# The passage from the first attention to its FFN in a written order on three engines: the context's part first, four modulation rows moved into the FFN

## The chip, the cores and the metric

The kernel runs on one core of a Trainium2 chip. The metric is the device time of one execution in microseconds (us); less is better. A run of the kernel on the chip gives one time; the time of a kernel is the median of its runs. A profiled execution is a further one, with its own time.

The engines of the core that matter here: PE (TensorE, matmuls into the PSUM memory; PEld is its weight load), DVE (VectorE), ACT (ScalarE), POOL (GpSimd) and SP (SyncE, which issues most transfers). Each works through its own queue in order, and engines wait for one another by semaphores.

## What is computed

A trunk of two layers over 512 latent tokens (x) and 256 context tokens (ctx) of width 1024. Cut to what matters:

```
for layer in range(2):
    mod_x = six vectors of 1024 from silu(c) @ ada_w[layer] + ada_b[layer]
    mod_c = six vectors of 1024 from silu(c_ctx) @ ada_w[layer] + ada_b[layer]
    h = rmsnorm(x) * (1 + mod[1]) + mod[0]          # for x and for ctx
    o = attention(h)                                # concatenated heads @ w_out
    x = x + mod_x[2] * o_x ;  ctx = ctx + mod_c[2] * o_c
    h = rmsnorm(x) * (1 + mod[4]) + mod[3]          # for x and for ctx
    x = x + mod_x[5] * ((silu(h_x @ w1) * (h_x @ w3)) @ w2)
    ctx = the same with h_c and mod_c[5]            # in layer 0 only
return rmsnorm(x) * final_g
```

The change touches layer 0 between `o = attention(h)` and the first products with w1 and w3.

## The kernel before

Activations lie transposed: a tile has 128 of the 1024 features on the partitions and the tokens along the free axis, so x is eight tiles of 128x512 (`xr`) and the context eight of 128x256 (`cr`). Every factor of a large product is split into a high and a low part, `hi` and `lo = src - hi`, and the product is three matmuls per 128 features (`mm3`, L209 to L211): high by high, high by low, low by high. The normalised inputs are `hx[k]` and `hc[k]`, each with its two parts (`xh`, `xl`, `ch`, `cl`); together they are `hb`. A weight tile of 128x1024 is loaded by SP (`raw`), copied to its high part by ACT (L160) and subtracted for the low part by DVE (L161); there are three buffers each of raw, high and low tiles. The class `Stream` (`S`) keeps the weights in one list and loads and splits them in that order, some ahead of their use.

Most of the program is put in order on the engines by the framework's scheduler: it takes the instructions in the order in which the program names them as a priority, and lets a later one go first on an engine that would otherwise stand still. `tc.issue_after` puts one instruction behind another on its engine. In a region of `manual_schedule` the named engines keep the written order of the region's instructions; the kernel before has one such region, at its start (lines 76 to 961).

**The end of the attention.** The attention's results of the eight units pass through `prep(m)`, which splits them into `hx[m]` and `hc[m]` (L1291, L1292, and `split`, L198 and L199, for the context). The output projection with `wo_ab` is done in two halves of four features tiles each. The first half (`first_part`, `wo_chunk(.., 0)`) lies among the attention's steps. The second half, `wo_chunk(m, w, "x" or "c", 4)` for m from 0 to 7, is twelve matmuls into one of two PSUM buffers (`lin`) and then one DVE instruction that adds the result times mod[2] to the residual (L1313). In the kernel before the x chunks come first, with the context's chunks of m = 0 and 1 among them, and the other six chunks of the context (`held`) after the x norm.

**The norms.** `sq_sum` squares the eight tiles on ACT (L331, L334) and adds them up in two accumulators, on DVE (L340) for even and on POOL (L338) for three odd ones. `rstd_of` sums over the features by a matmul with ones (L308), and makes 1/sqrt by Ln, Exp and a Newton step on ACT and DVE (L315 to L320). `h_make` makes one tile of the input of the FFN: a DVE product (L352), ACT's high part with the shift (L353), DVE's low part (L354).

**The modulation rows.** `ada_rows` makes one 128-feature piece of a modulation vector from a row tile of 128x1024 (512 KB, loaded by SP): two DVE instructions with a running sum (L271, L272), one for x and one for the context. In layer 0 the vectors 2 to 4 and the first half of vector 5 are made in the attention, four of these rows (vector 5, k = 0 to 3, `late_rows`) in this passage; the second half of vector 5 and all of layer 1 follow in the FFN through `rows(n, after)`, with two row buffers that SP fills again as they come free (`ada_request`, L623). Vector 5 is first used by the residual sums of the FFN (`to_residual`, L1553).

**The start of the FFN.** `plain_tile(0)` runs 16 small matmuls without use for the result (`keep_busy`, L219), and then w1 and w3 of the first 128 hidden features: x with w1, x with w3, then the context with both, each 8 x 3 matmuls. The table of ACT's functions is changed to Silu behind the context's last tile (`silu_tables`, L291). The FFN works on 22 hidden tiles: four plain ones (p = 0 and 1, two each), and nine pairs by a scheme of seven products in place of eight (`seven`, L1518 to L1520), with sums of tokens and weights that DVE makes (`token_sums`, `first_sum`), and the products with w2 (`down`, L1559 to L1561).

## Time and profile before

| | us |
|---|---|
| median of 3 runs (1594.85 to 1597.19) | 1596.67 |
| the profiled execution's own time | 1602.4 |
| its span, first to last instruction | 1600.6 |
| PE busy / DVE busy / ACT busy / POOL busy in the span | 1546.4 / 1245.5 / 738.3 / 261.2 |
| the passage and the first FFN tile in the span | about 420 to 487 |

How to read the lines that follow. A row of the timeline gives the start (us from the span's start), the time that it took, engine, line of the kernel, operation, `out<-in` by tile names, the shapes and the count, and in brackets how long the engine stood idle before it and for whom it waited. A row of a group gives line, engine, operation, names, shapes, count, then busy us and mean ns of one. A row of the windows gives from:to, the length, busy us (and count) of PE, PEld, DVE, ACT and POOL, the granted clock of PE (1.00 is full speed), the share of the 16 DMA engines and GB/s. Matmuls are pipelined: a matmul of 512 columns is shown with 0.39 us, while the next starts 0.23 us after it.

### The profile page before, as it was taken

The numbers are of one execution on the slowest core, as the hardware profiler recorded it, in microseconds if no ns is written. First come the engines' busy times: TensorE is split into PE (matmuls) and PEld (weight loads), VectorE is DVE, ScalarE is ACT, GpSimd is POOL, SyncE is SP. The second block draws the span as 40 slices with busy tenths as digits, with TensorE's granted clock in tenths as the row PEclk, the third lists the DMA queues.
The fourth block names the chain that finished last, engine by engine and source line by source line (L and its number), as shares of the span: only waits on it lengthen the run. The fifth ranks groups of instructions, "written<-read, shape, count | busy, mean of one in ns | idle before, by whom it ended". The sixth has DMA issues, their size and how long they took to land.

```text
span 1600.6 us, 25584 instructions
## 1 busy us (share of the span) xinstructions
PE 1546.4 (97%) x9904; PEld 1381.6 (86%) x9904; DVE 1245.5 (78%) x2135; ACT 738.3 (46%) x1280; POOL 261.2 (16%) x303
## 2 busy tenths in 40 slices
PE   8899998999999999999999999998998999999997
PEld 5798887877878999989999998886777899989896
DVE  4768797966698799879788867677766987869686
ACT  4546554445344423423424254456664543525354
POOL 1032223463010000000100001253431000000001
PEclk9999999999999999999999999999999999999998
DMA  9322253542245465575866752320002342423321
GB/s 357 105 60 81 77 166 125 182 139 87 63 132 158 119 182 158 135 208 160 213 180 165 200 148 71 106 67 27 28 27 65 120 145 72 130 73 96 119 80 53
DMA packets 68449, 195.28 MB, mean 122 GB/s; under 512 B 6772, under 2 KB 19220, under 8 KB 68328
## 3 DMA queue, kind: packets, MB, share of 16 engines
q1 hardware_dynamic: 58136, 159.95, 30.8%
q0 software_dynamic: 9184, 32.39, 9.6%
q8 instruction: 78, 1.28, 0.3%
q10 hardware_dynamic: 1008, 1.31, 0.2%
q14 instruction: 43, 0.35, 0.1%
HBM read 160.45 MB, written 4.86 MB: 103 GB/s over the span
## 4 chain that ended last, share of the span: by engine, by line
PE 58%; DVE 6%; DMA 3%; issue 2%; ACT 1%; POOL 0%; DVEq 0%; ACTq 0%; POOLq 0%; SPq 0%
PE f L1520 4%; PE f L1519 4%; PE f L1518 4%; PE f L1950 4%; PE f L1949 4%; PE f L1948 4%; PE f L1561 3%; PE f L1560 3%; PE f L1559 3%; PE f L210 3%; PE f L211 3%; PE f L209 3%; PE f L2001 2%; PE f L2002 2%; PE f L2003 2%
## 5 line engine op out<-in xcount | busy, mean ns | idle before, releaser
L198 ACT ACTIVATE wh<-raw 128x1024 fp32r<-128x1024 f32 (+1 forms) x96 | 92.3, 978 | 232.1 <-DVE raw L539 99.4
L209 PE MATMUL lin<-hb,wh 128*128 128x512 f32 (+1 forms) x440 | 157.2, 358 | 6.0 <-ACT hb L1291 3.1
L210 PE MATMUL lin<-hb,wh 128*128 128x512 f32 (+1 forms) x440 | 154.8, 352 | 0.5 <-DVE hb L1292 0.5
L211 PE MATMUL lin<-hb,wl 128*128 128x512 f32 (+1 forms) x440 | 154.4, 351 | 0.0
L199 DVE TENSOR_TENSOR wl<-raw,wh 128x1024 fp32r<-128x1024 f32 (+1 forms) x96 | 107.2, 1123 | 36.3 <-ACT wh L198 34.2
L271 DVE SCALAR_TENSOR_TENSOR junk<-raw,tables 128x1024 bf16<-128x1024 f32 x80 | 100.0, 1250 | 18.4 <-DMA raw<-in_ada_wT_dram 18.1
L204 POOL DMA_DIRECT2D wl<-raw x39 | 34.1, 874 | 445.3 <-ACT wl L203 388.4
L1559 PE MATMUL f<-g,wh 128*128 128x512 f32 (+1 forms) x304 | 102.8, 339 | 0.0
L1560 PE MATMUL f<-g,wh 128*128 128x512 f32 (+1 forms) x304 | 102.8, 339 | 0.0
L1949 PE MATMUL f<-hb,wh 128*128 128x256 f32 x360 | 101.7, 283 | 0.0
L1948 PE MATMUL f<-hb,wh 128*128 128x256 f32 x360 | 101.4, 283 | 0.0
L1950 PE MATMUL f<-hb,wl 128*128 128x256 f32 x360 | 101.2, 283 | 0.0
L1561 PE MATMUL f<-g,wl 128*128 128x256 f32 (+1 forms) x304 | 100.8, 336 | 0.2 <-DMA wl<-raw 0.2
L209 PEld LDWEIGHTS lin<-hb,wh 128*128 128x128 f32 x440 | 83.2, 189 | 20.4 <-ACT hb L1291 3.5
L1520 PE MATMUL f<-hb,wl 128*128 128x384 f32 x288 | 96.3, 334 | 0.2 <-DMA wl<-raw 0.2
L1518 PE MATMUL f<-hb,wh 128*128 128x384 f32 x288 | 96.3, 334 | 0.0
L1519 PE MATMUL f<-hb,wh 128*128 128x384 f32 x288 | 96.2, 334 | 0.0
L210 PEld LDWEIGHTS lin<-hb,wh 128*128 128x128 f32 x440 | 83.3, 189 | 11.1 <-DVE hb L1292 0.6
L211 PEld LDWEIGHTS lin<-hb,wl 128*128 128x128 f32 x440 | 83.3, 189 | 10.4
L161 DVE TENSOR_TENSOR wl<-raw,wh 128x1024 fp32r<-128x1024 f32 x57 | 74.0, 1300 | 16.0 <-ACT wh L160 14.0
L160 ACT CAST wh<-raw 128x1024 fp32r<-128x1024 f32 x57 | 59.7, 1050 | 57.0 <-PE t L210 15.0
L338 POOL TENSOR_TENSOR ns_a<-ns_a,ns_s 128x256 f32<-128x256 f32 (+1 forms) x12 | 12.2, 1018 | 420.8 <-ACT ns_s L334 414.2
(442 smaller groups left out, 4870.9 us busy)
## 6 DMA issues: line engine op xcount, KB each, us to landing
raw<-in_w_dram SPq DMA_DIRECT2D x132, 512.0 KB, 3.6
raw<-in_ada_wT_dram SPq DMA_DIRECT2D x80, 512.0 KB, 3.9
wl<-raw POOLq DMA_DIRECT2D x39, 512.0 KB, 6.3
raw<-in_w_ab_dram SPq DMA_DIRECT2D x24, 512.0 KB, 4.2
raw<-in_ada_w_dram SPq DMA_DIRECT2D x12, 512.0 KB, 9.3
raw<-in_w_c_dram SPq DMA_DIRECT2D x12, 512.0 KB, 3.7
nb<-in_na_bias_dram POOLq DMA_DIRECT2D x16, 256.0 KB, 3.3
raw<-in_wo_ab_dram SPq DMA_DIRECT2D x8, 512.0 KB, 3.5
```

Of the source, the lines that this page charges most:

```text
L209: nc.tensor.matmul(ps, wh(k), xh(k), start=k == 0, stop=False)
L210: nc.tensor.matmul(ps, wh(k), xl(k), start=False, stop=False)
L211: end = nc.tensor.matmul(ps, wl(k), xh(k), start=False, stop=k == n - 1)
L1518: nc.tensor.matmul(ps, wh(k), b[:, 0, :], start=k == 0, stop=False)
L1519: nc.tensor.matmul(ps, wh(k), b[:, 1, :], start=False, stop=False)
L1520: nc.tensor.matmul(ps, wl(k), b[:, 0, :], start=False, stop=k == 3)
L1559: nc.tensor.matmul(ps, hi, g[:, 0, cols[v]], start=first, stop=False)
L1560: nc.tensor.matmul(ps, hi, g[:, 1, cols[v]], start=False, stop=False)
L1561: nc.tensor.matmul(ps, lo, g[:, 0, cols[v]], start=False, stop=last)
L1948: nc.tensor.matmul(ps, wh(k), b[:, 0, :], start=k == 0, stop=False)
L1949: nc.tensor.matmul(ps, wh(k), b[:, 1, :], start=False, stop=False)
L1950: nc.tensor.matmul(ps, wl(k), b[:, 0, :], start=False, stop=k == 3)
```

## The change

1. The second half of the projection, both norms, the making of all sixteen `h` tiles and the matmuls of the first FFN tile stand in one region of `manual_schedule` for PE, DVE and ACT: on these three engines the written order holds. POOL and SP are not in it.
2. The order on PE: context chunks 0 to 5, x chunks 0 to 3, context chunks 6 and 7, x chunk 4, the context's norm matmuls, x chunks 5 to 7, the x norm's matmuls, then the first FFN tile with the context first and tile by tile (w1 and w3 in turn for each k), then x the same way. The context's norm and its eight `h` tiles lie among the last x chunks on DVE and ACT.
3. Each weight tile is split at a written place (`S.next(0)`), the two of the first FFN tile (`w00`) among the last x chunks.
4. All squares are added on DVE; POOL adds none. Of x the last square goes into the matmul as a third term in place of an addition.
5. The 16 small matmuls (`keep_busy`) are gone.
6. The four rows of vector 5 (k = 0 to 3) leave the passage. All eight rows of that vector now come in the FFN: four behind the passage, as before (k = 0 to 3 in place of 4 to 7), and two behind each of the two plain tiles of p = 1, which are new there.
7. ACT's Silu table is loaded after the last x tile.

```diff
-    ada1 = [(0, 5, k) for k in range(KT // 2, KT)] + [(1, z, k) for z in range(6) for k in range(KT)]
+    ada1 = [(0, 5, k) for k in range(KT)] + [(1, z, k) for z in range(6) for k in range(KT)]
...
-        rows = [(s_, k) for s_ in range(2, 6) for k in range(KT)]
+        rows = [(s_, k) for s_ in range(2, 5) for k in range(KT)]
...
-        held = []
-        for t in range(4):
-            w = S.next(3)
-            for m in (2 * t, 2 * t + 1):
-                wo_chunk(m, w, "x", 4)
-                if t:
-                    held.append((m, w))
-                else:
-                    wo_chunk(m, w, "c", 4)
-            late_rows[t]()
...
-        r = rstd_of(tp(), sq_sum(xr, nmap), D, nmap)
-        for k in range(KT):
-            h_make(k, hx[k], xr[k], r, 0, 1, 0, nmap)
         weights0()
-        for m, w in held:
-            wo_chunk(m, w, "c", 4)
...
+        ffn_start.enter_context(tc.manual_schedule(engines={ENG.PE, ENG.DVE, ENG.Activation}))
...
+        def part(t, *which):
+            for v in which:
+                for m in (2 * t, 2 * t + 1):
+                    wo_chunk(m, wos[t], v, 4)
+                    square(m, "xc".index(v))
+
+        def square(k, v):
+            xk, a = ((xr, cr)[v])[k], accs[v]
+            if k < 2:
+                nc.scalar.activation(a[k], xk, AF.Square)
+                return
+            sq = nmap[v].tile([P, (NX, NC)[v]], F32, tag="ns_s", name="ns_s")
+            nc.scalar.activation(sq, xk, AF.Square)
+            if (k, v) == (KT - 1, 0):
+                a.append(sq)
+            else:
+                nc.vector.tensor_add(a[k % 2], a[k % 2], sq)
...
+        for t in range(2):
+            wos[t] = S.next(0)
+        part(0, "c")
+        wos[2] = S.next(0)
+        part(1, "c")
+        part(2, "c")
+        part(0, "x")
+        wos[3] = S.next(0)
+        part(1, "x")
+        part(3, "c")
+        w00 = [S.next(0)]
+        wo_chunk(4, wos[2], "x", 4)
+        rstds[1] = rstd_of(tp(), accs[1], D, nmap[1])
+        square(4, 0)
+        wo_chunk(5, wos[2], "x", 4)
+        h_t(0, 1)
+        square(5, 0)
+        h_t(1, 1)
+        h_lo(0, 1)
+        w00.append(S.next(0))
+        wo_chunk(6, wos[3], "x", 4)
+        h_t(2, 1)
+        h_lo(1, 1)
+        h_t(3, 1)
+        square(6, 0)
+        h_lo(2, 1)
+        wo_chunk(7, wos[3], "x", 4)
+        square(7, 0)
+        h_lo(3, 1)
+        h_t(4, 1)
+        psx = tp()
+        for i, a in enumerate(accs[0]):
+            nc.tensor.matmul(psx, ones, a, start=i == 0, stop=i == 2)
+        h_t(5, 1)
+        h_lo(4, 1)
...
+        h_t(0, 0)
+        h_lo(6, 1)
+        h_t(7, 1)
+        h_t(1, 0)
+        h_lo(0, 0)
+        h_lo(7, 1)
+        for k in range(2, KT):
+            h_t(k, 0)
+            h_lo(k - 1, 0)
+        h_end = h_lo(KT - 1, 0)
+        nc.scalar.preload_act_table_set("silu_and_others")
...
-                keep_busy(ps[0][0], 16, before[0])
-                w = [[wslice(z) for z in S.next(1 - i)] for i in range(2)]
-                for c in range(2):
-                    for i in range(2):
-                        mm3(ps[i][c], *w[i], *((ch, cl) if c else (xh, xl)))
+                w = [[wslice(z) for z in t] for t in w00]
+                for c, h, l in ((1, ch, cl), (0, xh, xl)):
+                    for k in range(KT):
+                        for (wh, wl), o in zip(w, ps):
+                            nc.tensor.matmul(o[c], wh(k), h(k), start=k == 0, stop=False)
+                            nc.tensor.matmul(o[c], wh(k), l(k), start=False, stop=False)
+                            nc.tensor.matmul(o[c], wl(k), h(k), start=False, stop=k == KT - 1)
+                ffn_start.close()
...
-        rows(4, h_made[-1][1])
+        rows(4, h_end)
...
                     for i in range(2):
-                        plain_tile(2 * p + i, g)
+                        end = plain_tile(2 * p + i, g)
                         if i and not p:
                             token_sums()
+                        if p:
+                            rows(2, end)
```

Between the matmuls into `psx` and `h_t(0, 0)` stand the x norm's Ln, Exp and Square on ACT and its three DVE steps, with `h_lo(5, 1)` and `h_t(6, 1)` among them. `h_t(k, v)` is the DVE product and ACT's high part of tile k (v is 0 for x and 1 for the context), `h_lo(k, v)` DVE's low part.

More of the change, by code (lines that the diff above doesn't have):

```diff
@@ L221, in keep_busy @@
                 nc.tensor.matmul(ps[:, 0:P], ident, ones, start=True, stop=True)
-    before = [None]
     def wo_slices(t, i):
@@ L1256, in f @@
                 junk = rp.tile([P, NX], F32, tag="ru", name="junk", bufs=1).bitcast(mybir.dt.bfloat16)
-                raw = S.next()
-                if s_ < 5:
-                    return ada_rows(0, s_, k, [tables, rbuf], raw, junk)
-                with tc.issue_after(last_sum[0].ins):
-                    ada_rows(0, s_, k, [tables, rbuf], raw, junk)
+                ada_rows(0, s_, k, [tables, rbuf], S.next(), junk)
             out_ = []
@@ L1369, in tile_trunk @@
-        r = rstd_of(tp(), sq_sum(xr, nmap), D, nmap)
-        for k in range(KT):
-            h_make(k, hx[k], xr[k], r, 0, 1, 0, nmap)
-        weights0()
-        for m, w in held:
-            wo_chunk(m, w, "c", 4)
-        nmap = PoolMap(
-            ns_a0=(sp, "k1", 2), ns_a1=(sp, "k1", 2), ns_s=(sp, "v", 2), ns_h=(sp, "q", 2),
-            ns_v=(sp, "k1", 2), ns_y=(sp, "k2", 1), ns_t=(sp, "v", 2),
-        )
-        r = rstd_of(tp(), sq_sum(cr, nmap), D, nmap)
-        for k in range(KT):
-            act = h_make(k, hc[k], cr[k], r, 0, 1, 1, nmap)
@@ L1383, in tile_trunk @@
-        silu_tables = act_tables("silu_and_others", act)
+        weights0()
+        ffn_start.enter_context(tc.manual_schedule(engines={ENG.PE, ENG.DVE, ENG.Activation}))
+        nmap = [
+            PoolMap(
+                ns_a0=(ap, "at", 2), ns_a1=(ap, "at", 2), ns_s=(ap, "p", 5), ns_h=(ap, "p", 5),
+                ns_v=(ap, "at", 2), ns_y=(ap, "at", 2), ns_t=(ap, "p", 5),
+            ),
+            PoolMap(
+                ns_a0=(sp, "k1", 2), ns_a1=(sp, "k1", 2), ns_s=(sp, "v", 2), ns_h=(sp, "q", 2),
+                ns_v=(sp, "k1", 2), ns_y=(sp, "k2", 1), ns_t=(sp, "v", 2),
+            ),
+        ]
@@ new lines, in tile_trunk @@
+        accs = [[nmap[v].tile([P, n], F32, tag=f"ns_a{e}", name="ns_a") for e in range(2)] for v, n in enumerate((NX, NC))]
+        wos = {}
+        def part(t, *which):
[14 more added lines that the diff above has]
+                nc.vector.tensor_add(a[k % 2], a[k % 2], sq)
@@ new lines, in tile_trunk, with h_t, h_lo @@
+        made = {}
+        def h_t(k, v):
+            n, r = (NX, NC)[v], rstds[v]
+            t = nmap[v].tile([P, n], F32, tag="ns_h", name="ns_h")
+            nc.vector.scalar_tensor_tensor(t, (xr, cr)[v][k], amod[0][:, 1, v, k : k + 1], r, op0=ALU.mult, op1=ALU.mult)
+            nc.scalar.activation((hx, hc)[v][k][:, 0, :], t, AF.Identity, bias=mod[0][:, 3, v, k : k + 1], scale=1.0)
+            made[k, v] = t
+        def h_lo(k, v):
+            h = (hx, hc)[v][k]
+            return nc.vector.scalar_tensor_tensor(
+                h[:, 1, :], made[k, v], mod[0][:, 3, v, k : k + 1], f32(h[:, 0, :]), op0=ALU.add, op1=ALU.subtract
+            )
@@ new lines, in tile_trunk @@
+        h_lo(0, 1)
[15 more added lines that the diff above has]
+        h_lo(4, 1)
+        nv, ny, nt = (nmap[0].tile([P, NX], F32, tag=z, name=z) for z in ("ns_v", "ns_y", "ns_t"))
@@ new lines, in tile_trunk @@
+        nc.scalar.activation(nt, psx, AF.Ln, bias=epst, scale=1.0 / D)
+        nc.vector.tensor_scalar(nv, psx, 1.0 / D, EPS, op0=ALU.mult, op1=ALU.add)
+        h_lo(5, 1)
+        nc.scalar.activation(ny, nt, AF.Exp, scale=-0.5)
+        h_t(6, 1)
+        nc.scalar.activation(nt, ny, AF.Square)
+        nc.vector.scalar_tensor_tensor(nt, nt, -0.5, nv, op0=ALU.mult, op1=ALU.mult)
+        nc.vector.scalar_tensor_tensor(ny, nt, 1.5, ny, op0=ALU.add, op1=ALU.mult)
+        rstds[0] = ny
+        h_t(0, 0)
```

26 lines of the change are left out of this document (8 added, 18 removed).

## The prediction

> **What bounds the kernel now.** I read the page first, then the passage by windows, PE's timeline in it, the groups by shape, and the waits of PE over the whole span.
>
> ```profile
> span 1600.6 us, 25584 instructions
> PE 1546.4 (97%) x9904; PEld 1381.6 (86%) x9904; DVE 1245.5 (78%) x2135; ACT 738.3 (46%) x1280; POOL 261.2 (16%) x303
> ```
>
> PE is the bound of the whole: 97% of the span. So the change can gain only where PE stands still or does work of no use. In the passage (windows; columns from:to, length, busy PE, PEld, DVE, ACT, POOL, clock, DMA share, GB/s) that is in one place:
>
> ```profile
> 450.00:460.00 10.00, 10.00 (x73) 8.99 (x74) 9.54 (x16) 7.00 (x12) 2.26 (x3) 1.00 0.37 107
> 460.00:470.00 10.00, 7.46 (x43) 5.93 (x43) 10.00 (x17) 4.79 (x10) 0.55 (x2) 1.00 0.76 265
> ```
>
> From 460 to 470 DVE is full and PE is not: there the passage is bound by DVE. PE's timeline says what PE loses:
>
> ```profile
> 430.46 0.40 PE L209 MATMUL lin<-hb,wh 128*128 128x512 f32 x1
> ...
> 441.14 0.39 PE L211 MATMUL lin<-hb,wl 128*128 128x512 f32 x1
> 442.64 0.47 PE L209 MATMUL lin<-hb,wh 128*128 128x512 f32 x1 [1.11 <-DVE res L1313]
> ...
> 453.04 1.88 PE L308 MATMUL t<-ns_a,ones 128*128 128x512 f32 x4
> ...
> 459.06 3.73 PE L219 MATMUL f<-ones,ident 128*128 128x128 f32 x32
> 463.52 1.10 PE L308 MATMUL t<-ns_a,ones 128*128 128x256 f32 x4 [0.73 <-DVE ns_a L340]
> 464.85 0.98 PE L209 MATMUL f<-hb,wh 128*128 128x512 f32 x3 [0.23 <-ACT hb L353]
> 467.40 0.50 PE L210 MATMUL f<-hb,wh 128*128 128x512 f32 x1 [1.58 <-DVE hb L354]
> ```
>
> The waits in brackets are 1.11 + 0.73 + 0.23 + 1.58 = 3.65 us, the small matmuls of L219 3.73 us: 7.4 us. That is the most that the change can take away; from 467.40 on the timeline shows PE without a gap.
>
> **The yardstick.** Between the first two of these rows lie 48 matmuls, so one of 512 columns takes (441.14 - 430.46)/47 = 0.227 us of PE; one of 256 columns takes 0.12, by the chain of waits:
>
> ```profile
> 481.88 0.12 PE f L209
> ```
>
> At 467.40 three of the 48 x matmuls of the first FFN tile are done: 45 x 0.227 + 48 x 0.12 = 16.0 us are left, so PE reaches the end of that tile's work at 483.4 in effect (it does it mixed with the second tile). I lay out the written order by hand, with durations of rows, and ask when the same work ends.
>
> ```profile
> L271 DVE SCALAR_TENSOR_TENSOR junk<-raw,tables 128x1024 bf16<-128x1024 f32 x8 | 9.7, 1218 | 2.9 <-DMA raw<-in_ada_wT_dram 2.9
> ...
> L161 DVE TENSOR_TENSOR wl<-raw,wh 128x1024 fp32r<-128x1024 f32 x6 | 7.3, 1220 | 0.5 <-ACT wh L160 0.5
> L160 ACT CAST wh<-raw 128x1024 fp32r<-128x1024 f32 x6 | 6.3, 1050 | 8.3 <-PE lin L210 3.7 <-DMA raw<-in_wo_ab_dram 2.3 <-PE f L210 2.2
> ...
> L1313 DVE SCALAR_TENSOR_TENSOR res<-lin,mod,res 128x512 f32<-128x512 f32 x8 | 5.9, 745 | 3.1 <-PE lin L211 3.1
> ...
> L353 ACT ACTIVATE hb<-ns_h,mod 128x512 fp32r<-128x512 f32 x8 | 5.6, 719 | 5.3 <-DVE ns_h L352 5.3
> L352 DVE SCALAR_TENSOR_TENSOR ns_h<-res,amod,ns_y 128x512 f32<-128x512 f32 x8 | 5.5, 744 | 0.0
> ...
> L334 ACT ACTIVATE ns_s<-res 128x512 f32<-128x512 f32 x6 | 3.8, 632 | 11.9 <-DVE res L1313 11.9
> ...
> L353 ACT ACTIVATE hb<-ns_h,mod 128x256 fp32r<-128x256 f32 x8 | 3.7, 504 | 4.6 <-DVE ns_h L352 4.6
> ...
> L352 DVE SCALAR_TENSOR_TENSOR ns_h<-res,amod,ns_y 128x256 f32<-128x256 f32 x8 | 3.5, 480 | 0.0
> ```
>
> On one engine the next instruction starts about 0.08 us before the one ahead ends, so DVE needs 0.66 for 512 columns, 0.40 for 256 and 1.14 for a weight tile; across engines I add 0.05 us. An addition of squares:
>
> ```profile
> 448.55 0.69 DVE L340 TENSOR_TENSOR ns_a<-ns_a,ns_s 128x512 f32<-128x512 f32 x1 [0.76 <-ACT ns_s L334]
> ```
>
> **The start.** The context's chunks come first, and they need `hc[7]`, the last thing that the attention makes:
>
> ```profile
> 420.34 0.69 DVE L1236 COPY pt<-t 128x512 f32<-128x512 f32 x1 [0.39 <-PE t L1234]
> ```
> ```profile
> 424.06 1.08 PE L410 MATMUL t<-pt,v 128*64 128x256 f32 x8
> 425.08 0.50 PE L209 MATMUL lin<-hb,wh 128*128 128x512 f32 x1
> ```
>
> Before, x chunks cover this wait (the next row is one). Now L410 can start when its copy ends, at 421.1, and ends at 422.2; ACT's copy and cast and DVE's subtraction, 0.4 us each with their latencies, give `hc[7]` at 423.5. PE does nine matmuls of context chunk 0 meanwhile and ends it at 423.8. Five more context chunks at 12 x 0.12 = 1.44, four x chunks at 12 x 0.227 = 2.73 and two context chunks: 423.8 + 10.1 + 10.9 = 444.8. One wait is on the way: the third weight tile's subtraction (1.14) stands on DVE ahead of the sum of context chunk 2, chunk 4 needs that chunk's PSUM buffer, and PE waits 0.9. With 0.3 for restarts and a short wait x chunk 4 starts at 446.0, ends at 448.7; the context's norm matmuls (1.10, the L308 row) and three x chunks (8.2) follow: **PE ends x chunk 7 at 458.1**, 0.9 us ahead of the 459.06 at which it ended its chunks before.
>
> **Where DVE stands then.** This is the step on which I decide. Three times in the written order DVE waits for ACT while PE's sums are due, each time 1.2 us:
> - 452.5: DVE begins the addition of x square 4, then the sum of x chunk 5 and context tile 0's product, to 454.2. ACT does that tile's high part (0.50) and only then square 5 (0.63). DVE adds it from 455.35.
> - To 456.75 DVE does the product of tile 1 and the low part of tile 0. ACT does tile 1's high part, then the copy of w3 (1.05). DVE subtracts it from 458.0 to 459.1. Only then comes the sum of x chunk 6, whose matmuls ended at 455.4.
> - Three context steps to 461.0; ACT: high part of tile 3, then square 6. DVE adds it from 462.15, then a low part, then **the sum of x chunk 7 at 463.2**, 5.0 us after PE ended it.
>
> Square 6 is added at 462.8: the x norm's matmul begins there, PE has stood still for **4.8 us**. Square 7 (0.63) is ready at 464.6, the third term runs (0.4 more of waiting), and the result is there at 465.5. Ln, Exp, Square on ACT with a context tile between, two DVE steps: 469.7. The last context low part stands on DVE behind six more instructions and ends at 473.0; the FFN's context part, 48 x 0.12 = 5.8 us, which should cover this, waits for the last two tiles (1.1 + 0.2 + 1.0) and ends at 473.7. x follows at 48 x 0.227 = 10.9, with DVE just fast enough (2 x 0.66 = 1.32 for a tile against 6 x 0.227 = 1.36): **484.6**. Against 483.4: **+1.2 us**. So the 7.4 us are given back as new waits of PE: 0.2 + 0.9 + 4.8 + 0.4 + 2.3 and restarts. With latencies of 0 to 0.08 across engines the same schedule ends from 483.3 to 485.6: from -0.1 to +2.2.
>
> **The clock.** The small matmuls go, and nothing fills the 4.8 us. Elsewhere in this span PE stood still as long:
>
> ```profile
> PE t L1189 <- DVE ns_v L316: 4.1, 1, 4.1
> ```
> ```profile
> 278.00:279.00 1.00, 1.00 (x9) 1.00 (x8) 1.00 (x3) 0.60 (x2) 0.00 (x0) 0.67 0.06 16
> 279.00:280.00 1.00, 1.00 (x7) 1.00 (x7) 1.00 (x2) 0.67 (x2) 0.00 (x0) 0.50 0.21 66
> 280.00:281.00 1.00, 1.00 (x6) 1.00 (x6) 1.00 (x5) 0.00 (x0) 0.00 (x0) 0.50 0.98 225
> 281.00:282.00 1.00, 1.00 (x8) 1.00 (x7) 1.00 (x3) 0.54 (x1) 0.00 (x0) 0.62 0.56 225
> ```
>
> That wait ended at 277.7, and the clock was at half for the best part of four windows; the sum of what was missing, 0.33 + 0.50 + 0.50 + 0.38, is 1.7 us of PE. Here it would fall on the x norm's matmul (1 us later on DVE's chain) or on the context part, which waits anyway (0), or on the x part (1.7). I take +0.8, of 0 to 1.7. The Trainium skill, page "TensorE: Matmul & The Clock Gate", section "HAM oscillation", allows no idle gap of PE above about 3.4 us; by that rule alone the clock falls here, and the case has the price above. The trace agrees with its 4.1 us.
>
> **The rows.** Four rows are 8 DVE instructions of 1.22: 9.8 us leave the passage (counted above by their absence) and come back behind the two tiles of p = 1, with four loads of 512 KB in SP's queue among the FFN's weights. There:
>
> ```profile
> 530.00:540.00 10.00, 10.00 (x66) 9.88 (x65) 8.13 (x15) 6.21 (x9) 0.00 (x0) 1.00 0.33 107
> 540.00:550.00 10.00, 10.00 (x59) 9.73 (x58) 7.79 (x16) 5.68 (x8) 2.59 (x3) 1.00 0.68 149
> 550.00:560.00 10.00, 10.00 (x59) 8.77 (x58) 3.23 (x7) 2.44 (x3) 0.00 (x0) 1.00 0.65 167
> ```
>
> DVE is free for 1.9 + 2.2 + 6.8 = 10.9 us in these 30, just enough. The holes near the end do not help what is due at 545: two rows (4.9) less the 1.9 make `first_sum` 3 us late, and the product on it. PE has products with w2 at hand at that place, so I take +0.5, of 0 (all hidden) to 3 (none); below zero has no reason, since PE has no gap to lose there. The POOL additions that DVE now does are in the schedule. The Silu table lies behind 480 on ACT, where nothing is late: 0; without the second FFN tile as cover it would cost its load on the way to the first Silu.
>
> **The sum.** +1.2 + 0.8 + 0.5 = +2.5 us. The profiled execution's own time is 1602.4 (span and 1.8 around it), 5.7 above the median of the runs; it would become 1604.9, and the median 1596.67 becomes 1599.2; I say 1599.0. A difference of 0.2%, 3.2 us, is about what a measurement of this kernel can tell from no change.
>
> **Rivals.**
> - *Slower: the clock stays low into the x part, and `first_sum` comes 3 us late.* After the long gap come three more short ones while PE is half idle from 458 to 474. If a second stretch at half clock falls on the x part (1.7), the first on the norm (1.0), and the rows stall PE by 1 to 3: 1.2 + 2.7 + 2 = +6, 1602.7. For it: the rows at 278. Against: from 464.85 to 467.40 PE did little and the clock stayed 1.00. It decides from the point where the gap exceeds about 4 us.
> - *Faster: the three waits of DVE are not there*, because ACT's steps fall elsewhere than I lay them. Each hole closed brings 1.2, all three 3.6, and the end of the gap takes the clock term with it: 1.2 - 3.6 - 2.3 (the context part in time) + 0.5 = -4.2, 1592.5.
> - *The order is not what it says.* In the first region the scheduler puts later work into a written order:
>
> ```profile
> 74.02 1.22 DVE L161 TENSOR_TENSOR wl<-raw,wh 128x1024 fp32r<-128x1024 f32 x1
> ```
>
> L161 there lies between the two steps of L891 and L892. Here the subtraction of the next FFN weight could slip in after 458: 0 if it falls into a hole, +1.1 on the chain if not: 1599 to 1601.
>
> **How the numbers follow.** Forecast 0.46, slower rival 0.20, faster rival 0.22, the order filled up 0.12. The forecast alone reaches from -0.1 to 2.2 + 1.7 + 3 = +6.9 if all bounds meet; 0.28 of it I put within 3.2 us, 0.18 above. Same: 0.28 + 0.02 (faster rival, small) + 0.08 (filled up) = 0.38. Slower: 0.18 + 0.20 + 0.04 = 0.42. Faster: 0.20. The range leaves out a tenth on each side: below 1592.5 half of the faster rival, above 1604.5 the worst of the slower one.
>
> **What would show it.** Right: DVE's sum of x chunk 7 some 5 us after PE's last matmul of it, a wait of PE of 4 to 5 us in front of the x norm's matmul, a clock below 1.00 behind it, DVE waits of about 1.2 for ACT at the squares 5 and 6 and at the copy of w3, and the end of the first FFN tile near 484. Wrong: that wait below 2 us, or PE through the first tile before 480; then the passage gains. For the rows: a wait of PE between 533 and 560, where there is none now.

## The result, and the profile after

| | before | after |
|---|---|---|
| median of five runs, us | 1596.67 | 1605.5 |
| range of the runs, us | 1594.85 to 1599.38 | 1603.13 to 1611.48 |
| profiled execution: own time / span, us | 1602.4 / 1600.6 | 1608.45 / 1606.7 |

The ratio is 1.0055, with a 95% interval of 1.0034 to 1.0075: the change makes the kernel 8.8 us slower. The prediction had 1599.0 with a range to 1604.5; slower was its likeliest sign, but by far too little.

To see where the 8.8 us arose, I take three points at which PE has done the same work in both kernels: the last transposes of the attention, the first product of the seven-product scheme (by then all four plain tiles are done), and the last product with w2. In PE's timeline of the kernel before these are

```profile
419.26 0.93 PE L1234 MATMUL t<-ident,pc 128*128 128x128 f32 x7
...
533.53 0.34 PE L1518 MATMUL f<-hb,wh 128*128 128x384 f32 x1
...
985.85 0.28 PE L1561 MATMUL f<-g,T 128*128 128x256 f32 x1
```

and in that of the kernel after (its lines: L1306 is the sum of a chunk into the residual, L1371 and L1375 a square and its addition, L1382, L1383 and L1388 the three steps of an `h` tile, L1425 the x norm's matmuls, L1569 the Silu, L269 and L270 the two instructions of a row, L1582 to L1584 the seven products, L1623 to L1625 the products with w2, L1617 their sum into the residual; in the other kernels these numbers are up to 30 higher, in kernel 2 up to 3 lower than in the kernel before)

```profile
413.99 1.04 PE L1234 MATMUL t<-ident,pc 128*128 128x128 f32 x8
...
452.70 0.39 PE L211 MATMUL lin<-hb,wl 128*128 128x512 f32 x1
458.77 3.36 PE L1425 MATMUL t<-ns_a,ones 128*128 128x512 f32 x4 [5.69 <-DVE ns_a L1375]
461.54 0.71 PE L209 MATMUL f<-hb,wh 128*128 128x256 f32 x1
...
463.40 1.02 PE L1425 MATMUL t<-ns_s,ones 128*128 128x512 f32 x2
...
533.39 0.69 PE L1582 MATMUL f<-hb,wh 128*128 128x384 f32 x1 [2.10 <-ACT q L1569]
...
990.24 0.28 PE L1625 MATMUL f<-g,T 128*128 128x256 f32 x1
```

The first stretch, the passage and the plain tiles, grew from 533.53 - 419.26 = 114.3 us to 533.39 - 413.99 = 119.4: +5.1, of which the 2.10 us in the bracket at 533.39 are a wait directly ahead of the seven-product scheme, and 3.0 lie in the passage. The second, the rest of the FFN, grew from 452.3 to 456.9: +4.5. Together they are 9.7 us. (The attention ahead of the first point took 5.3 us less than in the profile of before, which had the 4.1 us wait at 277; the same place costs 0.9 us in the changed kernel and 1.2 in kernel 2 below, so that wait is not the change's.) There is one profile of each kernel. The part ahead of the first point takes from 410.7 to 419.7 us in the fourteen profiles of this text, the part behind the last from 614.3 to 618.0 (614.7 before, 616.5 after); a difference of one or two us between two profiles can be chance, and the medians of the runs decide on the whole.

The passage, by windows (columns as in the prediction):

```profile
440.00:450.00 10.00, 10.00 (x49) 8.28 (x48) 6.89 (x13) 4.64 (x9) 0.00 (x0) 1.00 0.18 54
450.00:460.00 10.00, 4.31 (x16) 2.97 (x15) 7.75 (x14) 4.32 (x7) 0.00 (x0) 0.91 0.41 132
460.00:470.00 10.00, 9.68 (x61) 7.72 (x60) 4.79 (x10) 3.61 (x7) 0.00 (x0) 0.92 0.20 79
```

and in steps of two microseconds, with the clock in the third column from the right:

```profile
458.00:460.00 2.00, 1.23 (x2) 0.74 (x3) 2.00 (x5) 0.28 (x1) 0.00 (x0) 0.55 0.91 350
460.00:462.00 2.00, 2.00 (x4) 0.73 (x4) 1.35 (x4) 1.26 (x3) 0.00 (x0) 0.60 0.97 387
462.00:464.00 2.00, 2.00 (x16) 1.76 (x14) 0.00 (x0) 0.00 (x0) 0.00 (x0) 1.00 0.00 0
```

PE, full in 450:460 before, works for 4.31 of these 10 us, and neither DVE (7.75) nor ACT (4.32) is full: both wait for one another. That is the gap of the hand schedule, 5.69 us in place of the 4.8 forecast, with half the clock behind it. DVE's own timeline shows the three waits of the forecast and one row that it had only as a rival:

```profile
450.03 0.69 DVE L1375 TENSOR_TENSOR ns_a<-ns_a,ns_s 128x512 f32<-128x512 f32 x1 [1.10 <-ACT ns_s L1371]
...
452.64 1.23 DVE L161 TENSOR_TENSOR wl<-raw,wh 128x1024 fp32r<-128x1024 f32 x1 [1.12 <-ACT wh L160]
453.78 0.75 DVE L1306 SCALAR_TENSOR_TENSOR res<-lin,mod,res 128x512 f32<-128x512 f32 x1
...
455.23 1.22 DVE L161 TENSOR_TENSOR wl<-raw,wh 128x1024 fp32r<-128x1024 f32 x1
...
457.94 0.69 DVE L1375 TENSOR_TENSOR ns_a<-ns_a,ns_s 128x512 f32<-128x512 f32 x1 [1.09 <-ACT ns_s L1371]
...
458.94 0.75 DVE L1306 SCALAR_TENSOR_TENSOR res<-lin,mod,res 128x512 f32<-128x512 f32 x1
```

The waits are 1.10, 1.12 and 1.09. The row at 455.23 is the subtraction for the second FFN tile's first weight, which the scheduler set into the written order. The sum of x chunk 7 (458.94) comes 6.2 us after PE's last matmul of it began (452.70).

In the FFN, the windows that answer to those of before:

```profile
530.00:540.00 10.00, 7.89 (x40) 7.69 (x39) 9.97 (x18) 6.17 (x11) 0.00 (x0) 0.83 0.34 107
540.00:550.00 10.00, 10.00 (x59) 9.69 (x58) 9.78 (x19) 6.44 (x9) 1.91 (x3) 1.00 0.86 194
550.00:560.00 10.00, 8.53 (x41) 6.73 (x41) 6.91 (x15) 1.34 (x3) 0.68 (x1) 1.00 1.02 320
```

DVE is full to 550 where it had 4 us to spare, and PE, full before, loses 2.1 and 1.5 us here. PE's waits between 415 and 1000 us (engine, line, tile, whom it waited for, us in total, times, longest):

```profile
PE t L1425 <- DVE ns_a L1375: 5.7, 1, 5.7
PE f L1582 <- ACT q L1569: 2.1, 1, 2.1
...
PE f L1623 <- DVE q L1607: 1.4, 1, 1.4
PE f L1583 <- DVE hb L199: 1.1, 1, 1.1
PE f L1558 <- DVE hb L1388: 0.9, 1, 0.9
PE lin L209 <- ACT hb L198: 0.9, 1, 0.9
PE lin L209 <- DVE res L1306: 0.8, 1, 0.8
PE f L1623 <- DVE s L1612: 0.6, 1, 0.6
PE f L1582 <- ACT hb L198: 0.4, 1, 0.4
```

L1583 waits for `first_sum`'s low part (L199), L1623 (the products with w2) for PSUM that DVE is late to empty. In DVE's timeline the last piece of `first_sum` is

```profile
553.06 1.22 DVE L270 SCALAR_TENSOR_TENSOR junk<-raw,csr 128x1024 bf16<-128x1024 f32 x1
...
554.20 1.02 DVE L199 TENSOR_TENSOR hb<-q,hb 128x384 fp32r<-128x384 f32 x2
```

behind the eighth of the row instructions; in the kernel before it was

```profile
544.75 1.50 DVE L199 TENSOR_TENSOR hb<-q,hb 128x384 fp32r<-128x384 f32 x3 [0.69 <-ACT hb L198]
```

So it ends at 555.2 where it ended at 546.2: 9 us late, not 3. (At 533.5 PE is at the same place in both profiles, so these times can be compared.)

### The profile page after: what moved, and what is told of

Its sections match the earlier page's. It is cut to its first block, busy times and chain, and to the rows that moved or that the text cites. A ratio compares the mean times of both kernels' runs of the same rounds, so it can differ in the third digit from the quotient of the medians.

```text
span 1606.7 us, 25518 instructions
## 1 busy us (share of the span) xinstructions
PE 1547.6 (96%) x9874; PEld 1380.5 (86%) x9874; DVE 1242.9 (77%) x2138; ACT 738.1 (46%) x1280; POOL 255.3 (16%) x299
## 4 chain that ended last, share of the span: by engine, by line
PE 54%; DVE 4%; issue 4%; DMA 3%; ACT 2%; POOL 0%; DVEq 0%; POOLq 0%; ACTq 0%; SPq 0%
PE f L1583 4%; PE f L1582 4%; PE f L1584 4%; PE f L2016 4%; PE f L2015 4%; PE f L2014 4%; PE f L1624 3%; PE f L1623 3%; PE f L1625 3%; PE f L2067 2%; PE f L2068 2%; PE f L2069 2%; PE t L408 2%; DMA wl<-raw 2%; PE t L1821 1%
## 5 line engine op out<-in xcount | busy, mean ns | idle before, releaser
L199 DVE TENSOR_TENSOR wl<-raw,wh 128x1024 fp32r<-128x1024 f32 (+1 forms) x96 | 107.0, 1119 | 35.2 <-ACT wh L198 32.4
L269 DVE SCALAR_TENSOR_TENSOR junk<-raw,tables 128x1024 bf16<-128x1024 f32 x80 | 98.5, 1232 | 16.8 <-DMA raw<-in_ada_wT_dram 16.4
L1623 PE MATMUL f<-g,wh 128*128 128x256 f32 (+1 forms) x304 | 103.2, 341 | 2.2 <-DVE q L1607 1.4
L1624 PE MATMUL f<-g,wh 128*128 128x512 f32 (+1 forms) x304 | 102.6, 339 | 0.0
L1625 PE MATMUL f<-g,wl 128*128 128x512 f32 (+1 forms) x304 | 101.1, 337 | 0.0
L1582 PE MATMUL f<-hb,wh 128*128 128x384 f32 x288 | 97.2, 338 | 2.5 <-ACT q L1569 2.1
L1583 PE MATMUL f<-hb,wh 128*128 128x384 f32 x288 | 96.9, 337 | 1.1 <-DVE hb L199 1.1
L1584 PE MATMUL f<-hb,wl 128*128 128x384 f32 x288 | 96.8, 336 | 0.0
L1584 PE MATMUL f<-T,wl 128*128 128x384 f32 x216 | 72.2, 334 | 0.0
```

The costliest lines, as they stand in the source:

```text
L1582: nc.tensor.matmul(ps, wh(k), b[:, 0, :], start=k == 0, stop=False)
L1583: nc.tensor.matmul(ps, wh(k), b[:, 1, :], start=False, stop=False)
L1584: nc.tensor.matmul(ps, wl(k), b[:, 0, :], start=False, stop=k == 3)
L1623: nc.tensor.matmul(ps, hi, g[:, 0, cols[v]], start=first, stop=False)
L1624: nc.tensor.matmul(ps, hi, g[:, 1, cols[v]], start=False, stop=False)
L1625: nc.tensor.matmul(ps, lo, g[:, 0, cols[v]], start=False, stop=last)
```

## The experiments

The theory after the result: two separate causes, the four rows in the FFN (4.5 us) and the written order of DVE and ACT in the passage (5 us). The rivals: the passage's loss is DVE's amount of work whatever the order; the rows cost their DVE time anywhere; the loss is the clock's; or what the scheduler sets into the region makes it.

All ratios are to the kernel before, run beside each. "First" is the stretch from the attention's last transposes to the first product of the seven, "second" from there to the last product with w2, both from the one profile of each kernel, at the same rows as above. An interval holds for the ratio alone.

| kernel | ratio (95% interval) | first, us | second, us |
|---|---|---|---|
| before | 1 | 114.3 | 452.3 |
| after | 1.0055 (1.0034 to 1.0075) | 119.4 | 456.9 |
| 1 rows left out | 1.0034 (1.0017 to 1.0052) | 119.5 | 450.6 |
| 2 only the rows moved | 1.0020 (1.0008 to 1.0032) | 113.3 | 457.0 |
| 3 rows early | 1.0044 (1.0032 to 1.0056) | 120.8 | 449.9 |
| 4 rows without their loads | 1.0068 (1.0042 to 1.0094) | 119.2 | 455.6 |
| 5 order repaired | 1.0022 (1.0008 to 1.0036) | 112.5 | 456.3 |
| 6 no second tile in the region | 1.0070 (1.0047 to 1.0093) | 118.1 | 460.8 |
| 7 small matmuls, 40 calls | 1.0083 (1.0061 to 1.0105) | 120.8 | 458.1 |
| 8 small matmuls, 22 calls | 1.0050 (1.0033 to 1.0067) | 116.4 | 459.6 |
| 9 order and rows | 1.0003 (0.9987 to 1.0019) | 114.8 | 449.9 |
| 10 and the norm early | 0.9994 (0.9979 to 1.0009) | 113.3 | 450.6 |
| 11 and another start | 0.9993 (0.9980 to 1.0006) | 112.1 | 450.8 |
| 12 and the rows spread | 0.9993 (0.9978 to 1.0009) | 111.1 | 450.6 |

The second stretch parts the kernels without an overlap: it is 449.9 to 450.8 us in the six that have no rows behind the tiles of p = 1 (1, 3, 9 to 12), 452.3 in the kernel before, and 455.6 to 460.8 in the seven that have the rows' DVE work there.

**1. The rows left out.**

```diff
-    ada1 = [(0, 5, k) for k in range(KT)] + ...
+    ada1 = [(0, 5, k) for k in range(KT // 2, KT)] + ...
...
+    nc.vector.memset(mod[0][:, 5, :, 0 : KT // 2], 0.5)
...
-                        if p:
-                            rows(2, end)
```

> The changed kernel without the four modulation rows behind the two tiles of p = 1: their loads and their 8 VectorE instructions are left out, the four entries hold a constant. Theory A (the rows are dear in the FFN: they delay the sum first_sum from 546 to 555 us and push loads of weights back, which the changed kernel shows as PE waits of 0.4 + 1.1 + 1.4 + 0.6 us between 552 and 623): these waits go, 1605.5 becomes about 1602. Theory B (my prediction: the rows cost 0.5 us, the rest of the FFN's loss comes from the passage, by way of the token sums that end 3.3 us late and the half clock behind the 2.1 us wait at 533): 1605. In both the wait of about 2 us at 533 stays, as the rows come behind it.

Measured: 1.0034 in place of 1.0055, 3.4 us less; the second stretch is 6.3 us shorter. PE's waits between 500 and 700 us are only two, the first of them half of what it was:

```profile
PE f L1583 <- ACT q L1570: 1.0, 1, 1.0
PE f L1624 <- DVE s L1613: 0.6, 1, 0.6
```

Theory A: the rows make the waits of 0.4, 1.1 and 1.4 us from 550 on, which are gone. The 0.6 us (L1624 here, L1623 in the changed kernel) stays, so it is not the rows'. The intervals of the two ratios overlap; what tells the kernels apart is the second stretch. The first is no shorter, although the wait ahead of the seven products is: behind the gap ahead of the norm the clock was at half for twice as long as in the changed kernel, from 458.4 to 465.2.

**2. Only the rows moved.** The kernel before, with the rows taken out of `late_rows` and put behind the tiles of p = 1, as in the change.

```diff
-                    if m >= 4:
-                        late_rows += row_pieces(1)
...
-            late_rows[t]()
...
-                        plain_tile(2 * p + i, g)
+                        end = plain_tile(2 * p + i, g)
...
+                        if p:
+                            rows(2, end)
```

> The kernel before with only the four rows moved into the FFN (behind the two tiles of p = 1); the passage is as before, 9.8 us of VectorE lighter. Theory A (rows dear in the FFN, 3 to 4 us): the passage gains at most its 3.65 us of waits and the FFN loses 3 to 4: 1596 to 1599, with PE waits between 550 and 565. Theory B (rows nearly free in the FFN): 1593 to 1596, no PE wait there.

Measured: 1.0020, 3.2 us slower. The first stretch gains 1.0 us from 9.8 us less of DVE's work (with half clock in it from 455.1 to 458.6, behind waits of 0.95 and 1.35 us), the second loses 4.6. New waits of PE stand where the change has them (L1556 is a product with w2):

```profile
PE f L1516 <- DVE hb L199: 1.3, 1, 1.3
PE f L1556 <- DVE q L1535: 1.0, 1, 1.0
...
PE f L1556 <- DVE q L1536: 0.9, 1, 0.9
```

These waits are 3.2 us; one of 1.6 us for a load (L1517, `wl<-raw`, at 668) is in the second stretch too, and the changed kernel does not have it. Theory A, from the other side: this one part of the change is slower by itself, and a little dearer than the expectation had it.

**3. The rows early.** Two rows among the attention's last chunks, two as single DVE instructions at x chunks 0 to 3.

```diff
+                    if m in (1, 3):
+                        early += row_pieces(1)
+                    if m in (6, 7):
+                        S.add(ada_wT[m - 4], "ada")
...
-        part(0, "x")
-        wos[3] = S.next(0)
-        part(1, "x")
+        row_half(2, 0)
+        wo_chunk(0, wos[0], "x", 4)
+        square(0, 0)
+        row_half(2, 1)
+        wo_chunk(1, wos[0], "x", 4)
+        square(1, 0)
+        wos[3] = S.next(0)
+        row_half(3, 0)
...
```

> The changed kernel with the four rows not in the FFN but early: two among the last attention's chunks (400 to 415 us), two as four single VectorE instructions, one at each of x chunks 0 to 3 of the passage, where VectorE is busy for 4.9 of 10 us. Theory A (the rows cost 3 to 4 us because VectorE and the weight queue are full at 530 to 560): like the kernel without these rows, 1.0034 of the kernel before in place of 1.0055, and PE's waits between 550 and 565 go. Theory B (a row costs its VectorE time wherever it stands): no gain against the changed kernel, 1.0055; then the x chunks wait for sums.

Measured: 1.0044, between the two expectations, and its interval overlaps with the change's. The second stretch is as short as without the rows (449.9), so in the FFN theory A holds. But DVE, with a row on each side of the fourth weight tile's split, was late for the sums of the x chunks, and PE waited 2.5 us for them, 1.7 more than in the changed kernel (the row of the changed kernel with L1306 had 0.8):

```profile
PE lin L209 <- DVE res L1306: 2.5, 3, 1.5
```

**4. The rows without their loads.** The 8 DVE instructions stay, on data that is there.

```diff
                         if p:
-                            rows(2, end)
+                            for k in (2 * i, 2 * i + 1):
+                                with tc.issue_after(end.ins):
+                                    ada_rows(0, 5, k, csr, csr[1], junk)
```

> The changed kernel with the 8 VectorE instructions of the four rows in their place behind the two tiles of p = 1, but on data that is in memory already: the four loads of 512 KB, and the use of these rows' values, are left out. Theory A (VectorE's 9.8 us make first_sum late): the PE waits at first_sum (0.4 + 1.1) and for its sums (1.4) stay, 1.005 to 1.0055 of the kernel before, like the changed kernel. Theory B (the four loads in the queue of the weights make pieces of weights late, as VectorE's 3.1 us wait for one at 557 to 560): most of the cost goes, 1.0034, like the kernel without the rows.

Measured: 1.0068, no less than the change itself (the intervals overlap); the second stretch is 455.6, 5.0 us above the kernel without rows. PE waits for DVE's sums again:

```profile
PE f L1624 <- DVE res L1618: 1.1, 1, 1.1
PE f L1624 <- DVE q L1598: 1.1, 1, 1.1
```

They stand at the products with w2, and none at `first_sum`, where theory A had them too. So it is DVE's time; the loads in the weights' queue cost 1.3 us at most in these profiles.

**5. The order repaired.** The same instructions; on ACT each x square goes ahead of the next context tile's high part, and is added one DVE step later; the sum of x chunk 7 and the norm's matmuls go ahead of the split of w3.

```diff
-        square(4, 0)
+        add4 = square(4, 0)
         wo_chunk(5, wos[2], "x", 4)
-        h_t(0, 1)
-        square(5, 0)
+        add5 = square(5, 0)
+        add4()
+        h_t(0, 1)
+        add5()
         h_t(1, 1)
         h_lo(0, 1)
-        w00.append(S.next(0))
         wo_chunk(6, wos[3], "x", 4)
+        add6 = square(6, 0)
...
+        w00.append(S.next(0))
         h_lo(3, 1)
```

> The changed kernel with another written order of the same instructions on VectorE and ScalarE: each x square stands on ScalarE ahead of the next context tile's high part and is added one VectorE step later, the sum of x chunk 7 and the norm's matmul come ahead of the split of the second FFN weight, and context tiles 3 to 7 follow them. Theory A (the gap ahead of the norm is made by the written order of the two engines): PE waits about 1 us ahead of the norm's matmul in place of 5.7, no drop of the clock, the norm ends 7 to 9 us earlier, and the kernel gains 5 to 9 us: 1597 to 1600. Theory B (VectorE has simply too much to do from 450 to 480, whatever the order): the wait moves behind the norm, the gain is under 2 us.

Measured: 1.0022, 5.3 us less than the change; the first stretch is 6.9 us shorter. PE's timeline has the norm's first two sums without a wait, 39.1 us after the attention's last transposes where they came after 44.8, and the third directly behind them:

```profile
452.14 1.96 PE L1423 MATMUL t<-ns_a,ones 128*128 128x512 f32 x4
453.94 1.02 PE L1423 MATMUL t<-ns_s,ones 128*128 128x512 f32 x2
```

The clock stayed at full. Theory A: the gap was the written order's, not DVE's amount of work. A wait of 2.7 us came up behind it, for the context's last tiles (`PE f L1561 <- DVE hb L1388`).

**6. No second tile in the region.** The split of the second tile's first weight is held behind the last DVE instruction of the region.

```diff
+                    if (i, j) == (0, 1):
+                        S.request(S.at + 3)
+                        with tc.issue_after(h_end.ins):
+                            S.make(S.at + 1)
```

> The changed kernel with the split of the second tile's first weight held back behind the passage's last VectorE instruction, so that neither this subtraction nor the 12 matmuls of the second tile stand ahead of the x norm's third sum. Theory A (what the scheduler slotted in lengthens the chain of the norm: 1.1 us on VectorE and 1.4 to 2.6 on PE): Ln comes 2.5 to 3.5 us earlier and the kernel gains 1 to 2 us, 1.0045. Theory B (it is work that PE has to do anyway, and without it PE stands still while the norm is made): Ln is earlier, PE waits longer behind it, 1.0055 to 1.0065.

Measured: 1.0070, not told apart from the change's 1.0055. The gap ahead of the norm is 4.7 us, as by the hand schedule, and Ln comes 9.8 us after x chunk 7's last matmul (450.05 to 459.88) where it came 11.8 after it; but PE waits 1.8 us for the last context tiles, and the second stretch grows by 3.9 with 3.9 us of waits for `first_sum` in place of 1.1, and the clock at half behind them from 551.1 to 557.9, which is 3.4 us of PE. The gain that theory A had for the total is not there. That what the scheduler set in was useful work in a gap, as theory B has it, fits, but this run doesn't show it by itself.

**7 and 8. Small matmuls in the gap,** with 40 and with 22 calls.

```diff
         psx = tp()
+        keep_busy(psx, 40)
```

> The changed kernel with 40 small matmuls on TensorE (4.7 us at the 0.117 us that the 32 of the kernel before took each) between x chunk 7 and the x norm's matmul, where it stands still for 5.7 us. They do no useful work and their result is written over. Theory A (half clock behind the gap makes the norm's three 512-column sums last about 5 us where they take 2.3 at full clock): the granted clock stays 1.00 there, the norm's first ScalarE step comes about 2.9 us earlier, and the kernel gains 2 to 3 us: about 1603. Theory B (the norm's lateness comes from VectorE alone, or the context part waits anyway for its own tiles): less than 1 us, 1605.

> The changed kernel with 22 calls of the small matmul in the 5.7 us gap; the earlier kernel with 40 calls showed that one call is two matmuls of 0.114 us, so that it filled 9.1 us, 3.4 more than the gap, and came out later. 22 calls are 5.0 us. Theory A (the half clock behind the gap costs): clock 1.00 at the norm's matmul, its first two sums take 1.3 us in place of 2.8, Ln comes 2 to 3 us earlier against the end of x chunk 7 (11.8 us behind it in the changed kernel), and the kernel gains 1.5 to 2.5 us, 1.004 to 1.0045. Theory B (the context part waits for its tiles anyway): Ln earlier, but under 1 us of gain, 1.005.

Measured with 40: 1.0083, slower. The clock stayed at 1.00, but a call is two matmuls, so they took 9.1 us and the norm's matmul began 8.9 us after chunk 7 in place of 5.8. The expectation had the size wrong, and this kernel says only that they hold the clock. With 22 calls, PE's timeline:

```profile
450.61 5.07 PE L221 MATMUL t<-ones,ident 128*128 128x128 f32 x44
456.37 1.98 PE L1426 MATMUL t<-ns_a,ones 128*128 128x512 f32 x4 [0.69 <-DVE ns_a L1375]
457.79 0.68 PE L209 MATMUL f<-hb,wh 128*128 128x256 f32 x1
```

The first two sums take 457.79 - 456.37 = 1.4 us in place of 461.54 - 458.77 = 2.8. That is the price of half the clock on the norm's chain, 1.4 us. The first stretch is 3.0 us shorter (1.5 of it from the wait ahead of the seven products, 0.6 in place of 2.1), but the second is 2.7 longer: PE waits 0.9 and 1.1 us at `first_sum`, the clock is at half behind these waits from 549.5 to 552.9, and smaller waits come later. The ratio, 1.0050, is not told apart from the change's, nor from what either theory had. So for the first stretch the rival "the loss is the clock's" holds in part: with the clock at full, 3.0 of the 5.1 us are not there. The gap makes the drop, and kernel 5, which has no gap, has neither.

**9. Order and rows.** Edits 3 and 5 in one kernel.

> The repaired order of VectorE and ScalarE (1.0022 of the kernel before by itself) and the rows early in one kernel. Theory A (two separate causes): the gains add up, 1.0022 less 0.0021 is 1.000, with no PE wait above 1 us between 545 and 565. Theory B (both meet in the same full stretch of VectorE at 490 to 560, so that one hides the other): 1.001 to 1.002.

Measured: 1.0003. Theory A: with both causes removed the change costs nothing that these runs can tell, and the gains add up (0.0033 by kernel 5 and 0.0021 by kernel 1 off 1.0055, 0.0052 found; with the 0.0011 of kernel 3 in place of the 0.0021 the sum would be 0.0044, which the interval allows too). Two of the rows now stand ahead of the first point; what they cost there the two stretches can't show.

**10. The norm early,** added to kernel 9.

```diff
         w00.append(S.next(0))
+        nc.scalar.activation(nt, psx, AF.Ln, bias=epst, scale=1.0 / D)
         h_lo(3, 1)
         h_t(4, 1)
+        nc.scalar.activation(ny, nt, AF.Exp, scale=-0.5)
+        nc.vector.tensor_scalar(nv, psx, 1.0 / D, EPS, op0=ALU.mult, op1=ALU.add)
...
```

> As the kernel with both repairs, and the steps of the x norm ahead of the context tiles 4 to 7: Ln directly behind the copy of the second FFN weight, both last steps of the norm ahead of context tile 6. With the repaired order alone Ln began at 458.97, 4 us after its matmul's end, because ScalarE did two weight copies and two high parts first, and PE waited 2.7 us at 462 to 465. Theory A (that wait is the written order's too): the norm ends 4 to 5 us earlier, the wait goes below 1 us, 2 to 3 us less than the kernel with both repairs, 0.998 to 0.999 of the kernel before. Theory B (VectorE has no room left, the last context tiles come late instead): the same time as with both repairs.

Measured: 0.9994. The wait of 2.7 us for the last context tiles fell to 0.4:

```profile
PE f L1584 <- DVE hb L1393: 0.4, 1, 0.4
```

The first stretch is 1.5 us shorter, the time 0.0009 less: the direction of theory A, about half its size, and inside what these runs tell apart.

**11 and 12. Another start, and the rows spread,** added to kernel 10: x chunk 0 and the third weight tile's split first, the row instructions behind context chunks 0 and 1 and x chunks 1 and 2; in 12 behind context chunks 0, 2 and 4 and x chunk 1, so that none follows the fourth tile's split. (One still stands right ahead of it, other than the expectation of 12 says.) The start of 12:

```diff
-        for t in range(2):
...
+        for t in range(3):
             wos[t] = S.next(0)
-        part(0, "c")
-        wos[2] = S.next(0)
...
+        chunk(0, "x")
+        chunk(0, "c")
+        row_half(2, 0)
+        chunk(1, "c")
...
```

> As the kernel with both repairs and the early x norm, with the start of the passage in another order: x chunk 0 first (it covers the wait for hc[7]), the split of the third weight tile ahead of it, and the single VectorE instructions of the two rows behind context chunks 0 and 1 and x chunks 1 and 2, in place of x chunks 0 to 3. PE's waits there were 0.9 (hc[7]), 0.8 (the subtraction of the third tile) and 1.7 us (the sum of an x chunk behind a row). Theory A (they are the written order's too): these 3.4 us go, and the kernel stands 2.5 to 3.4 us under the one without the new start: 0.9972 to 0.9978 of the kernel before. Theory B (the end of the passage is bound by VectorE, and what is gained at the start is waited for at the norm): 0.999.

> As the kernel with the new start, but the four single VectorE instructions of the two rows behind context chunks 0, 2 and 4 and x chunk 1, so that none stands beside the split of the fourth weight tile, which with a row on each side made PE wait 1.7 us at context chunk 6. Theory A (that wait is made by the place of the rows): it goes, 1.5 us less, 0.9983 to 0.9985 of the kernel before. Theory B (the end of the passage takes back what is gained at its start): 0.9993.

Measured: 0.9993 for both. In 11 only the 0.8 us wait went; the 0.9 for `hc[7]` stayed, because the attention's last product now stands behind x chunk 0 on PE, and so did the 1.5 at the row beside the split. In 12 that one went too. The first stretch fell to 112.1 and 111.1, by 1.2 of the 2.5 to 3.4 us that theory A had for 11, and by 1.0 of 1.5 for 12, and the second stretch took none of it back (450.8 and 450.6). For 11 the interval shuts out theory A's size. The medians show no part of the gain, but they could not: 1.2 and 2.2 us are 0.0008 and 0.0014, and the intervals are 0.0013 to 0.0016 wide to each side. So theory B isn't shown either. Kernels 10 to 12 are the fastest, but none is told apart from the kernel before.

## Why the prediction was wrong

**Right: the bound, and the passage by hand.** The waits 0.9 at context chunk 4 (measured 0.8) and 1.2 three times on DVE (1.10, 1.12, 1.09) are there, and so is the gap ahead of the x norm: 4.8 forecast, 5.69 measured, and 4.7 in kernel 6, where nothing is set into the written order. The waits for the last context tiles, 2.3 forecast, were 0.9 + 0.2. For the passage the forecast's terms were 1.2 + 0.8 = 2.0 us, the rival "the order is not what it says" added up to 1.1, and 3.0 were measured. That rival came true together with the forecast; I had given it a case of its own at 0.12, where it should have been a part of the likeliest case, since the trace of before showed that the scheduler does it. What the hand schedule could not show, and kernel 5 does: the order cost 7 us of the first stretch, and 5.3 of the median, that another order of the same instructions does not.

**Wrong: the term of the rows, "so I take +0.5".** This is the step that failed. It measured 4.5 us (the second stretch), 4.6 with the rows alone moved, and 5.0 to 6.4 between kernels that differ in them alone (4 and 1, after and 1, 5 and 9); in the medians kernel 2 lost 3.2. In the changed kernel 1.7 us of half clock lie at the start of this stretch, behind the wait at 533, but kernels 2 and 5 have full clock there and lose about as much, so the size doesn't hang on it. Two things in its working fell. First, "two rows (4.9) less the 1.9 make `first_sum` 3 us late": in the changed kernel all four rows, 8 instructions of 1.22, stand ahead of the last piece of `first_sum`, and DVE came to that place 3.3 us late already (its product for the first tile of p = 1 at 534.21, at 530.92 before). It was 9 us late. Second, "PE has products with w2 at hand": PE's queue has an order, and the products with w2 wait for PSUM that the same DVE has to empty. They were no cover, but waited themselves (1.4 us; the 0.6 later on is in kernel 1 too, without the rows). My own bound for no cover was 3; the bound had the wrong lateness in it.

**Missed: the wait ahead of the seven products.** The 2.10 us for the Silu at 533 were in no term. DVE's token sums ended 3.3 us late, Silu stands behind their copies on ACT, and PE needs the PSUM that Silu reads (the bracket names ACT's L1569). In the kernels with the changed passage it is 0 to 2.3 us. The rows of p = 1 are not its cause: they stand behind it, and it is 1.0 without them (kernel 1) and 0.8 with their DVE work (kernel 4). That it is shorter in these two than in the changed kernel is no gain: the longer half clock at 458 brought PE there later, and their first stretch is as long (119.5 and 119.2). Of the 3.3 us DVE's timelines show some 3: the token sums began 0.6 later, waited 0.7 longer for a load (1.94 at 508.27, 1.26 before), stood still for 0.8 at 522.97, and had a piece of `first_sum` (0.9, at 532.79) put ahead of their end. What brought these about was not tried by itself. Behind the wait the clock was at half once more (windows below), 1.7 us which the forecast had only once.

**The clock term** was within its bounds for the first gap of the changed kernel (0.8 of 0 to 1.7; 1.4 on the norm's chain). The bound was not safe: behind the same gap of 5.7 us the clock was at half for 6.8 us in kernels 1, 3 and 4, 3.4 us of PE. Nor does it decide from a gap of about 4 us, as the slower rival had it: 2.10 us at 533 was enough. How much of it reaches the end is open, since kernel 8, which saved the first drop, had another at 549.

The sum of what was measured, 3.0 + 2.1 + 4.5 = 9.6 us in the profiles, stands beside 8.8 of the medians; that they come so close is partly luck, as outside the two stretches the two profiles differ by -5.3 and +1.8 us. The slower rival (+6: low clock twice, and `first_sum` late) was nearest to what came, with the lateness taken at a third, and the second half clock on the x part and not, as it was, at 533.

## What to carry to other kernels

When work is moved off a full engine into a later stage, count all of it against the deadline in that stage: every instruction that lands ahead of what is due, and the lateness with which the engine arrives there; an average of free time over 30 us is no cover. A written order over several engines needs each pair of crossings laid out: put the producer's step on which the full engine's chain hangs (here ACT's square) ahead of its other steps, and let the consumer do one other step in between. And look for a gain of one stretch in the ones behind it: of kernel 8's 3.0 us in the first stretch 2.7 were lost in the second.

## What the runs showed of the hardware

The drop of the clock doesn't follow from the length of a wait alone. After the 2.10 us ahead of the seven products the changed kernel's clock was

```profile
533.00:534.00 1.00, 0.61 (x2) 0.61 (x3) 1.00 (x3) 1.00 (x3) 0.00 (x0) 0.65 0.00 0
534.00:535.00 1.00, 1.00 (x5) 1.00 (x4) 1.00 (x3) 0.55 (x1) 0.00 (x0) 0.50 0.00 0
535.00:536.00 1.00, 1.00 (x5) 1.00 (x4) 1.00 (x2) 0.75 (x1) 0.00 (x0) 0.50 0.00 0
536.00:537.00 1.00, 1.00 (x5) 1.00 (x5) 1.00 (x2) 0.10 (x1) 0.00 (x0) 0.65 0.00 0
```

while after 2.74 us in kernel 5 it stayed at full:

```profile
464.00:466.00 2.00, 0.88 (x7) 0.88 (x8) 2.00 (x4) 1.22 (x2) 0.00 (x0) 1.00 0.12 47
466.00:468.00 2.00, 1.84 (x12) 1.46 (x11) 2.00 (x5) 0.85 (x3) 0.00 (x0) 1.00 0.00 0
```

The Trainium skill, page "TensorE: Matmul & The Clock Gate", section "HAM oscillation — how this bites in real kernels", puts the limit at a gap of about 3.4 us; the drop after 2.10 us is against it, and the measurement decides.

What makes the difference can be read from the traces. In the windows above the clock was at half for (0.35 + 0.50 + 0.50 + 0.35)/0.50 = 3.4 us, from 533.3 on. Behind the norm's gap it was so for 3.4 us too, from 458.2 on, and between the two starts lie 75.1 us, which is 22 times 3.41. In each of the fourteen profiles all drops lie whole multiples of 3.41 us apart, and inside the span each lasts 3.41 or 6.83 us. So I divide the time into stretches of 3.41 us that end where a drop began (in kernel 5 counted from its drops at 61.0 and 1095.2). The stretch ahead of the changed kernel's drop, and then the two on which kernel 5's wait falls:

```profile
529.88:533.29 3.41, 1.40 (x12) 1.20 (x10) 3.38 (x9) 2.01 (x5) 0.00 (x0) 1.00 0.49 154
460.36:463.77 3.41, 2.02 (x17) 1.82 (x16) 2.14 (x4) 1.03 (x2) 0.00 (x0) 1.00 0.96 369
463.77:467.19 3.42, 1.91 (x12) 1.62 (x13) 3.31 (x8) 1.96 (x3) 0.00 (x0) 1.00 0.12 47
```

PE was busy for 1.40 us of the first, and for 2.02 and 1.91 of the others, since the border at 463.77 cut kernel 5's wait in two. From 400 to 1000 us the fourteen profiles have fourteen drops. Thirteen follow a stretch in which PE was busy for 1.70 us or less, one a stretch with 1.82; no stretch at full clock with 1.70 or less went without a drop, and those that did begin at 1.71. In this case, then, the drop comes when PE is busy for less than about half of such a stretch. Two waits that add up do it as well: 0.85 and 1.08 us in kernel 8 (busy 1.48). Where the borders lie against the program differs from profile to profile, so whether a wait of 2 to 3 us costs clock, and whether the gap of 5.7 us costs 1.7 or 3.4, is chance here. No run tried this by itself.
